# RWKV recurrence with split accumulator banks, low-rank weights scaled by halves, and a new instruction order

## The chip, the cores and the metric

The kernel runs on one core of a Trainium2 chip. The metric is the device time of one execution in microseconds (us); shorter is better. The core's engines are TensorE (PE in the profile, with PEld for its weight loads), VectorE (DVE), ScalarE (ACT), GpSimd (POOL) and SyncE (SP), which issues the transfers between device memory and the on-chip memory. Each engine works off its own queue in order; semaphores tie the queues together. Matrix products land in PSUM, which has eight banks of 512 float32 columns over 128 partitions.

## What is computed

A trunk of four residual layers works on x, 256 tokens by 1024 channels, in float32. Layers 0 and 3 mix tokens by RWKV-7, layer 1 by stick-breaking attention, layer 2 by sparse attention over selected keys; a SwiGLU feed-forward net follows each. The change touches the RWKV layers and the order of everything. Cut to what matters of the reference:

```python
shifted = jnp.pad(h, ((0, 0), (1, 0), (0, 0)))[:, :-1]
xm = h[:, :, None, :] + (shifted - h)[:, :, None, :] * mix
rkv = jnp.einsum('bsjd,jde->bsje', xm[:, :, :3], w_rkv)
logw = -jax.nn.softplus(-(w0 + jnp.tanh(xw @ w1) @ w2)) - 0.5
a = jax.nn.sigmoid(a0 + (xa @ a1) @ a2)
...
def step(state, inp):
    r_t, w_t, k_t, v_t, kk_t, a_t = inp
    sa = jnp.einsum('bhvk,bhk->bhv', state, kk_t)
    state = (state * w_t[:, :, None, :]
             - sa[..., None] * (kk_t * a_t)[:, :, None, :]
             + v_t[..., None] * k_t[:, :, None, :])
    return state, jnp.einsum('bhvk,bhk->bhv', state, r_t)
```

The step runs over 256 tokens in 16 heads of 64 channels.

## The kernel before

**A plan and a table.** The program isn't issued as it is written. `trunk` records every operation in a `Plan`; `schedule` (L478) then reads the order of all operations out of a packed table, `ORDER`, together with the engine of each operation that can run on two (those recorded on `anye`) and the buffer slot of each tile. `emit` (L526) issues them in that order, so that nearly every instruction of the profile has line L547. A turn 0 in the table stands for filler: two matmuls on a constant tile into a PSUM bank of their own, `warm_o` (L1571 to L1573). Unpacked, the table has 6579 turns, of which 35 are filler.

**Buffers.** Of the eight PSUM banks five have the tag `ps`, two the tag `g` (long products), and one is the filler's. Weights arrive in pieces of 512 KB in three buffers, `raw`. Most are split in two on arrival: ACT or DVE rounds a piece to `wh`, DVE subtracts to get the rest, `wl`, and products run over both parts.

**An RWKV layer.** In order of the code:

- The low-rank weights come by one transfer of 512 KB and one of 1536 KB into `lw` (L858). DVE scales the first by two vectors `mu`, 1024 columns each (L871 to L873), and the product `lora_in` runs over eight chunks of channels (L874).
- The sum of squares `ss` over x gives 1/rms (`rstd`). Then, for two chunks at a time, DVE forms h and one difference `dh` over both (L909 to L912), mixes, and the products follow: `kp` (keys), `rp`, `vp`, and the gate `pg`.
- The recurrence runs in four chunks of 64 tokens. Each chunk needs the inverse of a 64 x 64 triangular matrix per head and chunk. DVE inverts the 32 x 32 diagonal blocks (`inv`); transposes bring them to `xd` and `xw`, and four copies per layer go from `xw` into the tile `XT`, 64 columns wide. The lower left block is joined on TensorE in `combine` (L1184), four units per layer: a product into the bank `cmb1`, of which 32 + 32 partitions are copied to `zs` by two copies, and a second product into the bank `cmb2`, whose two halves go to `XT` with sign reversed. Both show as tile `cmb` in the profile.
- `Chain` (L1205) is the recurrence itself, for half of the heads, and is run twice. A step (L1212) is: `pS` (state times keys, two banks, not in the first chunk), DVE adds to `u`, `xu` (inverse times u, one bank), two evictions of 64 partitions each to `UV`, `qu` (update), DVE forms the new state `Sn`, and products into the output `Y`. The two halves of the heads are independent, so that the table can run them beside each other. Y of the second half holds two `ps` banks from its first step to its end. The norm of the output (`vb`) and the output projection (`po`) follow.

In the code, `halves` names the partitions 0 to 63 and 64 to 127: `r` is a half and `rb` the other one.

Of the kernel before, what the change touches and what calls it, by code (L numbers as in the profile page):

```python
# [303 lines left out]
8X(o*M@pQxAdc;WgQwPzs;|4cy1KgRSJj_pDf@3rzsC)(zHZu=qQ!1ZaMNzuZv&S%?WWzdn|9M~aQmj+v@cQPzcs^6yJ=sF{Bo0We&3Jl=7etAO}l9~?WT
PuLvUsDO`RfO371kqpP?Vr(o%0p(f87d56lw-Plyxg2vHFxj}{w7WF=x$+-<|zH*CkSxT$1D$y6knP0KWwzKHo&%ul#}G`8${mU3gBh$hAn*IgC1u-
&+83r`s4f%(-
Bgb`Io;)jMjjGML+rZj#m`s0rH#@3E7wv_Td+K^2t+_K?ROWO*Hv|54lrhJusz|ECc_tK8cpNgbBjvwa^3o>KK1Zfb7s<aZ*p|r>6rVuT8Xb3kNjr9zdJG
NbMJ-1}%6SkYNbFqo*em!m5e%6lLb}Z2z#g6TAq_Nj)NXz+E*0EcCv6iwUTjsA!vt@fZb2a<RnwiPu&42LL-M>#&)28AH6-yTi-
1lTOZLXwb@@LELPh}z^Gp@9L61OZFOPHP?mEIql5vde+B~JpAf`1%kasI~Pf|*aHV9)tG>??}B5d7iALw3$C*u&e8*gZz=ls+fNM1Jp(v3+`&?w&9<W^Bm
V4r9ktcAp)xO@>o!;ra#+@w|zbc-A1QQl`H0Hf~`FarKvodCcbi1rIS(!W1UyCxQMy)-i`3MsYcoLh49k-  # L310
bE9A*J8>n845GsU0$|UMSdmyvOt^8n0`veFdp|mRLEV!6?TE#3NsmoGRcgKgvpfmoJ6=wE;+!GyCfWPr6n{?vx^3!Vf@RJ9|&=@BoC4ABg5S(eT{K6W;kR
6#6DuTi(Ln|SGPK7ZDJdZrcrCKY8~scT&<R|f~7Sq7Ll!>UB|q@EFz}N<s{}4L(Hzm;|#5whZ#T0JtK}R?QSC4+_5|x6*H2Xk|A;?7&vLhunpj=f`V>NBI
Edh#a2w@c_l#b;>hOKvQ)-HrgjBzda~9n8C4a-HJr&4r?KkDWw}>?yjcX!(>(QnC-))2%9C=l%%JqJ-otJYMxFO!xE#SIx?5SSqYWn&B;{bWvnn@N<Si-l
QTGhQo|9^)Z2OTd))|=%jHk?2VD>0jP(iviNxMb35O#l`+!w6J<0v;xeAloT8lc7?DMSTVASDwmp@anSphKGTUEbt02Iq#+1*OIcE+yzqijELs%=u$rib+
7eMGu_A1?vgM_lbJSCJd0|zXTFD(b5K-
OJJ|~l#^q^kWK)^OW+frC)_~*VEZrh&;<3^E48nbf{COCUsb@xo*=<&q~%KZvdnz`shN+iXFgHdw%W9sfg^(!^};&w2{;Nm^)no^B4aE10bu}dO~SZlfCz
my!Kd#i=<YUxM-NF?4|*Grq+fazS|J(e+7u9{L&s<+d22o&0+Ko-ftGE^P**IW2i!KK=vQ3RZ3RiK3G=ij4A=2(0drk8LtRpVF0m1$d_R!21}-
>SEfYYcl(NZ+o+{IK%IkRvPico$c2b8z%%oVjS2W1o3*_dKm&n91j(N6k>9y@1SQZH~)+N|BqDksYv_%eij^ip5NXFG>LWnvxG{81t+hAaTSVc0yU51q`K
<S*pCkF(Sq?SMO)BYz~S$`5&eoT4&4T#D}?MIRGYBf^1SE*ELKdwBiRw}YwcK4tJ#pB|rIDB0ke0NaVd9|}Mv<KgY9jn`Y)z$5+`{v%Gd-wdiR_FHn%)Is
Fj(Pib=JW|WIypK%B3wVPVJ~j&9#p4RHa3ZkV&eJ8H2dJjy4$^%z3sE_8+=PyuGLKN`;7zJ|C{>lI=8-clCk*U^+9AO`OdVztCoM(RYON@sh-  # L320
!hS{=R>fwpUirmC{rP!{9y+Is?uJ2oejTHb~ZomQ^BDYMPu_s_D8Ms|HA`@LGEn#q^z<vg5>OQX`zE$+ai|EdpZ`~7D-
tk1R*+wZY9+idx;u@Si?+v^f*t~V8@WwAC|6EIY(yFIl6m)mA#T-
o2On60wc$gO*u*_v6)Om0UjWfPLwHE`l8Zzr;`tevlAGU|CuMVjV@GQf^>r0FtH2oyX_aM;!HFobU?$V<!;RNb=qs)edx0G9$!Y(`GdHK3yi=pAvnL4FY<
_iG#670y7y`7&iBz)i}RD+qX>#IbZ6*08iw!s0nWGn8R%8T%JS%mXiMX7kw`JjxCrQ-
E}?gOJHU{EZ^7h{xl}c*6Jn9s2m&zKX%nlQJTu18D%8#Vr_WINvWDI%qj19KwkMDJv8;<^~)a1n*Tw?u_D26N6Z)a^9wJI%N%VW}^q{jHYZ#NfOR`8sUL)
P8(R4J)+@^P+-WKjEOG0uK}Drr93x83Y36*4C0cYqAxWl33x`x4U}<dL6|%X0i>@@u+N_VACZs^G>-
9C2O2?kLj<|O?YD7z=l=t4H&}u(FXj=s%^b#Jj71H`<Q5Y#DiR{}5xKSynS_Y<G)*%JxLMrJ+4iwbb+v8R?Lx}NL`IUkW3+EXB8K549K$y(%QD8Rrm0;$8
w5Z%no&pyF4$kWSYkF>07g#ZdNGYg(g5_OPlZfGitmtZzs~S$%2N0vLrVMS@;y(Q5qMV!`6ti5={yxw`&*VcfB#(kh4{ccGmN|9&bxPn_~%bfrTEwuDr$<
Kh$(GF3FDS#Kcp+lo)T>_7GfyQg}B4G+^%$Pb>zDT#^&DR%_)W8_`z6?K59N#HF#eY%<3zCz>oIJ*=g$=YZsHrBQ;*j4l`!D+T*FyH%Bjz^55yK?LXPyH@
<C6i;vEE-fUzNelArxNoCeH8A~<yb}v&OPgrsU7g$SXy;FBP-AUtX(LUOHnw-  # L330
8yKCv4ke|UlS2AQ3++T+ujbpnr4N9Dtm$6H4L6TS>=kcVM^6oKy4E&XASobv~Edy;UPiFZEyz;5_2k{?H&rQur@Ua38YhimP`SH#)HSy2_Ke5G2i%d*DVx
_xl>01i^)<L2&Zb7Eyi$%DQH`CX{^N3b?{7P|xfY2%gGT4`+#w)R$QEpO7fAK&uI{r2=<*OQf;2W1Z`%Mo5HwW>|Nv76(6OZTAYFDeHs>(e|WGCa%H3TmC
zJtzCud5Hh06swDxX+&Z__=O=b^QS8rgXdE}jDR7X52Z9eCdhxSA`rJIMrvjx9bs$9;w4*c*Apww9aezYDT2Y={bRL%nmtqTU3;vGY#?3FKkL;BRS>yYYs
<^5Hj45#h<agAOL1-#@A^EJ1j926G3F|8Wzv!yBMkSz=6sbdX;d9(Y}6s5cIaXtvm7~|T9hS>dciPcnV-6@7>G-
# [1401 lines left out]
```

## Time and profile before

| what | value |
|---|---|
| median of 3 runs | 1362.21 us |
| lowest and highest | 1360.86 and 1362.78 us |
| the profiled execution's own time | 1363.01 us |
| its span in the profile | 1361.2 us |
| read from HBM | 217.08 MB, 160 GB/s over the span |

```profile
DVE  8999898776788988775799998876699998988754
ACT  5856467554235676554356865654249455666532
...
DMA  7332166655554557646646456666642421676554
```

Each digit is the busy share of one fortieth of the span (34 us) in tenths. The first RWKV layer takes the first five slices or so, the second one those from the thirtieth to the thirty-fourth. In both the transfers are light, at the end above all, and DVE is nearly full before the recurrence. Rows of a view by stretches give start and end, length, the busy time of PE, PEld, DVE, ACT and POOL with the count of instructions, the granted clock, the DMA share and GB/s. Rows of a timeline give start and length in us, engine, line, operation, out<-in; `x16` merges 16 instructions in a row. In square brackets stands how long the engine sat idle before and what ended it. Rows of a tile give shortest, median and longest duration in ns. A float32 matmul shows as two instructions, since TensorE takes it in two passes.

### The profile page before, as it was taken

To read this page: it belongs to the slowest core of one execution; us is meant where nothing else is said; L and a number is where in the kernel's file an instruction comes from. 1 tells how busy PE (TensorE), PEld (TensorE's weight loads), DVE (VectorE), ACT (ScalarE), POOL (GpSimd) and SP (SyncE) were. 2 spreads that over 40 slices of the span, in tenths; PEclk is the share of its full clock that TensorE was granted. 3 is DMA by queue.
4 is the path that set the end of the run, shared out by engine and by line. 5 is a ranking of instruction groups with operands and counts; after the bars stand their busy time and mean duration, and the time that the engine had idled before them with its cause. 6 is when DMAs were issued, how large, how long until landed. Compare 5 with 4: busy or idle time off the path is not lost.

```text
span 1361.2 us, 25699 instructions
## 1 busy us (share of the span) xinstructions
PE 1347.9 (99%) x10382; PEld 1179.9 (87%) x10382; DVE 1129.4 (83%) x1898; ACT 748.7 (55%) x1266; POOL 8.9 (1%) x18
## 2 busy tenths in 40 slices
PE   9999999999999999999999999999999999999998
PEld 8887898888888998888998788888898878988887
DVE  8999898776788988775799998876699998988754
ACT  5856467554235676554356865654249455666532
POOL 0000000000000000000000000000000000000000
PEclk9999999999999999999999999999999999999999
DMA  7332166655554557646646456666642421676554
GB/s 246 126 118 78 50 206 213 189 181 157 189 171 124 153 174 227 193 152 185 189 140 196 141 175 193 206 194 208 186 144 79 137 70 50 200 209 198 178 167 131
DMA packets 62854, 221.88 MB, mean 163 GB/s; under 512 B 7312, under 2 KB 8592, under 8 KB 62480
## 3 DMA queue, kind: packets, MB, share of 16 engines
q1 hardware_dynamic: 62736, 220.25, 52.2%
q8 instruction: 81, 1.33, 0.4%
q14 instruction: 37, 0.30, 0.1%
HBM read 217.08 MB, written 1.05 MB: 160 GB/s over the span
## 4 chain that ended last, share of the span: by engine, by line
PE 90%; DVE 4%; DMA 4%; ACT 1%; issue 1%; SPq 0%; DVEq 0%; ACTq 0%
PE gate L547 17%; PE dn L547 17%; PE up L547 17%; PE po L547 6%; PE qk L547 5%; PE vp L547 4%; PE kp L547 3%; DMA raw<-in_wts_dram 3%; PE rp L547 3%; PE vps L547 2%; PE z L547 2%; PE Y L547 1%; PE lora_in L547 1%; PE pg L547 1%; DVE wl L547 1%
## 5 line engine op out<-in xcount | busy, mean ns | idle before, releaser
L547 DVE TENSOR_TENSOR wl<-raw,wh 128x1024 fp32r<-128x1024 f32 x285 | 348.1, 1223 | 92.7 <-ACT wh L547 90.0
L547 ACT CAST wh<-raw 128x1024 fp32r<-128x1024 f32 x231 | 242.0, 1049 | 196.9 <-PE dn L547 110.5
L547 PE MATMUL dn<-h,wh 128*128 128x512 f32 x704 | 244.3, 390 | 0.0
L547 PE MATMUL dn<-h,wl 128*128 128x256 f32 x704 | 198.7, 282 | 0.2 <-DVE wl L547 0.2
L547 PEld LDWEIGHTS dn<-h,wh 128*128 128x128 f32 x704 | 132.2, 188 | 27.6
L547 PE MATMUL gate<-xg,wring 128*128 128x512 f32 x704 | 134.9, 336 | 0.8 <-DVE wring L547 0.5
L547 PEld LDWEIGHTS dn<-h,wl 128*128 128x128 f32 x704 | 133.1, 189 | 0.7 <-DVE wl L547 0.5
L547 PE MATMUL up<-xg,wring 128*128 128x512 f32 x704 | 132.2, 336 | 0.0
L547 DVE TENSOR_TENSOR wring<-raw,wring 128x1024 fp32r<-128x1024 f32 x88 | 107.6, 1222 | 29.6 <-ACT wring L547 27.2
L547 PE MATMUL gate<-xg,wh 128*128 128x512 f32 x352 | 125.5, 392 | 0.5 <-DVE gus L547 0.5
L547 PE MATMUL up<-xg,wh 128*128 128x512 f32 x352 | 125.4, 392 | 0.0
L547 PEld LDWEIGHTS gate<-xg,wring 128*128 128x128 f32 x704 | 107.4, 188 | 16.0 <-DVE wring L547 0.8
L547 PEld LDWEIGHTS up<-xg,wring 128*128 128x128 f32 x704 | 107.5, 188 | 14.6
L547 ACT CAST wring<-raw 128x1024 fp32r<-128x1024 f32 x85 | 89.3, 1051 | 46.1 <-DMA raw<-in_wts_dram 17.4
L547 PE MATMUL gate<-xg,wl 128*128 128x256 f32 x352 | 98.4, 280 | 0.0
L547 PE MATMUL up<-xg,wl 128*128 128x256 f32 x352 | 98.4, 280 | 0.0
L547 PE MATMUL qk<-xg,wh 128*128 128x256 f32 (+1 forms) x384 | 91.8, 320 | 0.0
L547 PEld LDWEIGHTS gate<-xg,wh 128*128 128x128 f32 x352 | 66.1, 188 | 15.3 <-DVE gus L547 0.8
L547 PEld LDWEIGHTS up<-xg,wh 128*128 128x128 f32 x352 | 66.1, 188 | 14.5
L547 PE MATMUL qk<-xg,wl 128*128 128x256 f32 x256 | 71.8, 280 | 0.4 <-DVE wl L547 0.3
L547 PEld LDWEIGHTS qk<-xg,wh 128*128 128x128 f32 x384 | 63.6, 188 | 6.3 <-issue 0.8
L547 PEld LDWEIGHTS gate<-xg,wl 128*128 128x128 f32 x352 | 66.1, 188 | 0.0
(325 smaller groups left out, 2620.5 us busy)
## 6 DMA issues: line engine op xcount, KB each, us to landing
raw<-in_wts_dram SPq DMA_DIRECT2D x397, 512.0 KB, 3.7
lora<-in_lora_dram SPq DMA_DIRECT2D x2, 1536.0 KB, 9.3
rhl<-qa SPq DMA_DIRECT2D x32, 64.0 KB, 3.1
xt<-in_xT_dram SPq DMA_DIRECT2D x4, 256.0 KB, 3.8
lora<-in_lora_dram SPq DMA_DIRECT2D x2, 512.0 KB, 4.8
lg<-in_lora_dram SPq DMA_DIRECT2D x8, 128.0 KB, 5.0
inv<-in_id_dram SPq DMA_DIRECT2D x2, 512.0 KB, 3.3
out_dram<-xt SPq DMA_DIRECT2D x4, 256.0 KB, 4.3
```

The lines of the kernel that those rows point to most:

```text
L547: getattr(getattr(nc, o.eng), method)(*map(real, args), **{k: real(a) for k, a in kw.items()})
```

## The change

1. `ORDER` is replaced; unpacked it has 6564 turns, 26 of them filler. Its positions in the table: 22 before the first real product (20 before), 2 and 2 in the two recurrences (5 and 10 before). Each transfer was given a wide margin when this order was sought.
2. The filler's own bank is gone: `ps` has six banks, and a filler turn writes to the `ps` bank that has been free longest. If none is free, the turn is left out.
3. The scaling of the low-rank weights runs in halves, four instructions of 512 columns instead of two of 1024, the first four chunks of channels first.
4. `dh` of the first two chunks is formed one by one.
5. The second transpose writes straight into the right half of `XT`; two copies per layer instead of four bring the upper blocks to the left half. `xw` is gone.
6. In `combine` the first product makes all 64 columns, so that one copy of 128 partitions replaces two of 32; the second product has a bank for each half.
7. `xu` has a bank for each half.

```diff
-        for o in ops:
+        left = {b: set(b.ops) for b in self.bufs if b.group == "ps"}
+        of, held = collections.defaultdict(list), {f"ps_{k}": (-1, None) for k in range(6)}
+        for b in left:
+            for o in b.ops:
+                of[o].append(b)
+        for n, o in enumerate(ops):
             if o is None:
-                warmer()
+                free = [(at, tag) for tag, (at, b) in held.items() if b is None]
+                if free:
+                    warmer(min(free)[1])
                 continue
+            for b in of[o]:
+                left[b].discard(o)
+                held[b.slot] = (n, b if left[b] else None)
...
-        for i in range(2):
-            m = mu[:, i].rearrange("p i c -> p c i")[:, :, :, None].to_broadcast([P, NC, 2, 64])
-            dve.tensor_tensor(w1a1[1 + i], w1a1[0], m, op=ALU.mult)
+        for c in range(0, NC, 4):
+            for i in range(2):
+                m = mu[:, i].rearrange("p i c -> p c i")[:, c:c + 4, :, None].to_broadcast([P, 4, 2, 64])
+                dve.tensor_tensor(w1a1[1 + i][:, c:c + 4], w1a1[0][:, c:c + 4], m, op=ALU.mult)
...
-            dve.tensor_tensor(dh[:, c:c + 2], h[:, c:c + 2, :S], h[:, c:c + 2, 1:], op=ALU.subtract)
+                if c == 0:
+                    dve.tensor_tensor(dh[:, i], h[:, i, :S], h[:, i, 1:], op=ALU.subtract)
+            if c > 0:
+                dve.tensor_tensor(dh[:, c:c + 2], h[:, c:c + 2, :S], h[:, c:c + 2, 1:], op=ALU.subtract)
...
-        xw = T([32, 32], "wh", "xw")
-        dve.transpose(xw.rearrange("p u t -> p t u"), XI)
-        for g in (1, 3, 0, 2):
-            r = slice(g * 32, (g + 1) * 32)
-            anye.copy(XT[r, :, g % 2 * 32:g % 2 * 32 + 32], xw[r])
+        dve.transpose(XT[:, :, 32:].rearrange("p u t -> p t u"), XI)
+        for r in (slice(0, 32), slice(64, 96)):
+            anye.copy(XT[r, :, :32], XT[r, :, 32:])
...
-            z, zs, z2 = bank("cmb1"), t1("zs"), bank("cmb2")
+            z, zs, z2 = bank("cmb1"), t1("zs"), (bank("cmb2"), bank("cmb2"))
...
-                        pe.matmul(z[hi:hi + 32, c * 32:(c + 1) * 32], SB[k][lo:hi, lo // 64, c0 + c // 4, c % 4, 0, 32:],
+                        pe.matmul(z[lo:lo + 64, c * 32:(c + 1) * 32], SB[k][lo:hi, lo // 64, c0 + c // 4, c % 4, 0, :],
                                   x[lo:hi, c], start=True, stop=True)
-            for hi in (32, 96):
-                anye.copy(zs[hi:hi + 32], z[hi:hi + 32, :S])
+            anye.copy(zs, z[:, :S])
...
-                        pe.matmul(z2[lo:hi, c * 32:(c + 1) * 32], zs[hi:hi + 32, c * 32:(c + 1) * 32],
-                                  xr_[hi:hi + 32, c], start=True, stop=True)
+                        pe.matmul(z2[lo // 64][lo:hi, c * 32:(c + 1) * 32], zs[hi:hi + 32, c * 32:(c + 1) * 32],
+                                  X[hi:hi + 32, c, 32:], start=True, stop=True)
             for lo in (0, 64):
-                anye.scale(X[lo:lo + 32, :, 32:], z2[lo:lo + 32, :S].rearrange("p (c t) -> p c t", c=2 * NCH), -1.0)
+                anye.scale(X[lo:lo + 32, :, 32:], z2[lo // 64][lo:lo + 32, :S].rearrange("p (c t) -> p c t", c=2 * NCH), -1.0)
...
-                a = bank("xu")
+                a = bank("xu"), bank("xu")
...
-                            pe.matmul(a[r, q * C:(q + 1) * C], XT[r, 4 * p0 + 4 * c + q, :], u0[r, q, :],
+                            pe.matmul(a[hh][r, q * C:(q + 1) * C], XT[r, 4 * p0 + 4 * c + q, :], u0[r, q, :],
                                       start=True, stop=True)
                 for hh, r, rb in halves:
-                    anye.scale(UV[hh][r, p0:p0 + 4, c, :], v3(a[r, :4 * C], 4), -1.0)
+                    anye.scale(UV[hh][r, p0:p0 + 4, c, :], v3(a[hh][r, :4 * C], 4), -1.0)
...
-    plan.emit(nc, {"ps": 5, "g": 2, "xm": XMS, "raw": RAWS, "wh": 3, "wl": 3, "t": TS, "t2": 5},
+    plan.emit(nc, {"ps": 6, "g": 2, "xm": XMS, "raw": RAWS, "wh": 3, "wl": 3, "t": TS, "t2": 5},
```

More of the change, by code (lines that the diff above doesn't have):

```diff
@@ L309 @@
[L309 to L334, printed above, removed]
@@ new lines @@
+cgg11Sy#8Km!wqCdOvm<;-Lw9&5%Q9ytKNM6N9DYp%C-
+D_UQg$AAyct4x)^6dOZuwJWi9ygtdp17_zyFG;5jn3rFMObJHB18tz0Z5|A=#6yeH(B1efCZb8d?lob#ugKe%<DKj8eF?rw8>cFIrq{wY7={DANAU7Em0d
+z<GQPdMM_7xdHP$9%0z<EP!X`A(0I&d>Sc1De@g!JF7YY|dc|{|Ot2Q&R(++Nu3L_OXIkLM$N8WA=wxoT<i$5r*_6#4Muip@a0>w4}n~H=0wzQn^x<V?n!
+-P<L$+Mk1hJ-+AekU6e&D?_$=;#<8EtWPrP80rP!iE)zDh1lNoSDF!!g9Lv9Y>n$e40poj&v7N6owmo7a>Q)D=-
+)C%|t*x;&m#wa>GP~Pl%NFY_;Ov}Y9oCv@wOO09db3eyY>GK@c7>JO{iQZ5HCYE)Ueubo2CHOQtppWj=R=kU$a;!pm_6q)0A(?$Gt`+w@JL+fGKfLJhAcC
+|3f!sl4{TktSlCwEN;EuA9=c3%atfgS%~)hQ87qR8CAFtj=Rr-
@@ new lines @@
+#zRx6ViA(flVkqE(@TVt)*c0%CJaP*RhN@>O!FZXV?>@-
+q#90DV{RFf}z#pY3x=znh^xZNTqn`hd82bEYF!UMzyy*LjQ~nBYyZ@Vj+w&&(3nRi(TtgR~h&nz}uxHDR2b_Df6)!CrDJf+zNsF5YXWof{3~iaLB})LE1p
+9u0Y&`@K`6Q&%C41*QP|D*~;<{|?jJ%^n8}lxpQBXij{HawV94?b`DlnbbkX0&!85v6UEi!G6@Cm>dr6u9JN(lR}#rqbeDbCAhj<CP+_)}q9u4P-
+|!@GCIKc872=-
+c9!5;xygUpx7Rke@nQ<SqF<VNvZNZwe*#kyw{P?TW4#(Rzb(vfvGIyLT+!pIMU!;>pUM=w39pn@d|?Z7$wXcN_hN>RIb8ad7nXK<|HDbej)$mTR^8uqNg{
+L3L8)YbTY~%F+Ilmi+o|xdHb_^{of^>D-
+{+>EFrC_R8|`ciYbnBsL%IHh1v1abfF0?hL2$eVoDd%E{W{+S3mY5E~D7z09_E;bE3Qe>Ujhg@2SkjPP*3i)U)*kZ*IQ*g($~#nz^?o?qK$IrdSO>BZmIO
@@ new lines @@
+<L4}4Btx;|Jyp5u{ARFMiT&(Q?FXJ>UGAcgs&K@h85`EZcG&(tUcN$h(aktxrFErMnvQX(xRce*!3xf#yO)BD8K0ll~$;;ePE>~u53{P5+JF>F}oT6~`37
+L@NPh;N8?ZfQTGK0)k#-NG+Y!|#B0Dq7NPq=#-
+{><TEc>~W<;clqyC(0UH1&gBY+r<B_7F1CQu}R6_t_|KJi%xaZvJMC(o`c%<@_8oTp%4=3ZLS!S;HKc?pq>)q@u6+oY=hR>)~33FO;e+!)lKq>NNps6OAO
+&*3cPD{*+G0n!~-g*;F;PnfomwG(d^qGcGAGLNyQiw+rS^EfvcCqEqrnvw>~>=(Z!%Ll<A{3KBp{NxKb9)r)AO49k3Q&l|&0yOQJVvlP-
+r$!dXJwd7btbW#QE-R~h(>hU0HD$X;vdeG=X22Td>ieWRK2RJ)(q(v{5)X*c<d7oLnyey&VsFyUdmNqUz|zRJw!YzuGPrW~-
+>SV$jS?*7KC3D@Iq#wIdMB%1IKuT=JV4SrU=<8_mvvHIYDA-=ljL?>g7Tx$7JF>pnqiQ?E*<-
@@ new lines @@
+=8GK3i{}EkUZCOTD}?<<%2>#oL=p!z;l*U*0Q5G&!5s#>RTQYC-IkX}lu;c?A57_U6B~B)i?9WvC=coQIEDKoS<mQYBDKH{3XwkY+YP5*Kt!`4*rcbfaKS
+6r4sF3WUj7npeun_xKb|&j6HQf|+!PnRU!E+++hxm_?-dGQ^WBOBtaxgeht$F(;NNCnb78>7PWi7;%Tm<^-%%XenaWytt;-
+Br%lCqCr7h(*h)eH2v`=B4H8`C&z*uxum#9>q()xl!l(RAVMK&OWHv)L<SRoG1xP{pLiN7O)4UV7~#RZ^8sT(6c<zV8g<erz}T!X(M@{Jm`qE62x&Vr%{(
+)!m`4-y`M*r#lT(1p^GJfptA5f;UnjkOU}G1-
+gndkUS5TL+OUaaZv6)JmPBtBLv^X($b3(`xm1AngW&%zoBtDd$dZJ!A8IU5Gn%ICz`4h3wXb>l$F_sup<|eQRIAJywQWBGinU1|R(RpIIV?7!&IrcHbDqb
+FuS&}Ey6CM0&rm<A%6ZA-
@@ L1570, in trunk @@
     nc.vector.memset(wx, 1.0)
-    wo = psum.tile([P, 512], F32, name="warm_o")
-    plan.emit(nc, {"ps": 5, "g": 2, "xm": XMS, "raw": RAWS, "wh": 3, "wl": 3, "t": TS, "t2": 5},
-              lambda: [nc.tensor.matmul(wo[:, :S], wx[:, :P], wx, start=True, stop=True) for _ in range(WARMERS)])
+    plan.emit(nc, {"ps": 6, "g": 2, "xm": XMS, "raw": RAWS, "wh": 3, "wl": 3, "t": TS, "t2": 5},
+              lambda tag: [nc.tensor.matmul(psum.tile([P, 512], F32, name="warm_o", tag=tag, bufs=1)[:, :S], wx[:, :P], wx, start=True, stop=True)
+                           for _ in range(WARMERS)])
 def _rows(w, r0, nr, c0, n):
```

79 lines of the change are left out of this document (41 added, 38 removed).

## The prediction

> **What bounds the kernel now.** I read the page first, then the busy times by stretch, then the waits, then the order of instructions at the places that the change touches.
>
> ```profile
> span 1361.2 us, 25699 instructions
> PE 1347.9 (99%) x10382; PEld 1179.9 (87%) x10382; DVE 1129.4 (83%) x1898; ACT 748.7 (55%) x1266; POOL 8.9 (1%) x18
> PEclk9999999999999999999999999999999999999999
> PE 90%; DVE 4%; DMA 4%; ACT 1%; issue 1%; SPq 0%; DVEq 0%; ACTq 0%
> ...
> 20.00:117.00 97.00, 97.00 (x795) 84.91 (x794) 94.74 (x187) 61.81 (x105) 4.37 (x5) 1.00 0.43 134
> 117.00:161.00 44.00, 42.84 (x1075) 33.50 (x1076) 37.95 (x85) 22.71 (x45) 0.00 (x0) 1.00 0.15 48
> ...
> 508.00:669.00 161.00, 161.00 (x931) 142.15 (x930) 120.82 (x163) 80.80 (x121) 0.00 (x0) 1.00 0.61 185
> ...
> 1100.00:1152.00 52.00, 50.32 (x1178) 39.69 (x1178) 43.99 (x93) 30.41 (x60) 0.00 (x0) 1.00 0.18 64
> ```
>
> TensorE is the bound nearly everywhere: 90% of the chain that ended last, never short of clock, and in a feed-forward stretch (508 to 669) not idle at all. No edit there can give anything unless it takes matmuls away, and this change takes none. What can be won is time in which TensorE waits or is fed filler. The stretches above (start and length, then busy time of PE, PEld, DVE, ACT, POOL) show two such places besides the start: the two recurrences of the RWKV layers, where PE lacks 44.00 - 42.84 = 1.16 us and 52.00 - 50.32 = 1.68 us. Beside this idle time stands the filler, matmuls on a constant tile:
>
> ```profile
> L1573 PE MATMUL warm_o<-warm_x x70: 272/273/421, 1.2 to 1130.9; 128*128 128x256 bf16 x70
> ...
> 1.20 6.73 PE L1573 MATMUL warm_o<-warm_x 128*128 128x256 bf16 x40 [1.20 <-DVE warm_x L1570]
> ...
> 1125.09 0.83 PE L1573 MATMUL warm_o<-warm_x 128*128 128x256 bf16 x6
> 1125.85 0.68 PE L547 MATMUL xu<-u,XT 64*64 64x64 f32 x16
> ```
>
> Forty of the 70 stand before the first real work, so 30, or 15 turns of two, lie in the recurrences. Six take 1125.85 - 1125.09 = 0.76 us, a turn thus 0.25 us and all 15 turns 3.8 us. With the idle time, 3.8 + 1.16 + 1.68 = 6.6 us is all that the two recurrences can give back without fewer matmuls.
>
> **The xu product in two banks.** Does it make TensorE faster?
>
> ```profile
> 106.55 10.63 PE L547 MATMUL vp<-xv,raw 128*128 128x256 f32 x48
> 117.11 0.71 PE L547 MATMUL qct<-consts,QC 64*128 64x64 f32 x16
> ...
> 143.37 0.46 PE L547 MATMUL pS<-Sn,PR 64*64 64x64 f32 x16
> 143.65 0.63 PE L547 MATMUL Y<-PR,Sn 64*64 64x64 f32 x16
> 144.12 0.63 PE L547 MATMUL xu<-QC,XT 64*64 64x64 f32 x16
> 144.61 0.68 PE L547 MATMUL xu<-u,XT 64*64 64x64 f32 x16
> ```
>
> From start to next start, 48 full passes of 256 columns take 117.11 - 106.55 = 10.56 us: 0.22 us each, so 0.055 us for 64 columns and 0.88 us for 16 passes in a row. One xu unit takes 0.49 us (144.12 to 144.61), so its two halves already run beside each other in one bank. pS, whose passes use all four pairs of partition halves, takes 0.28 us. The xu edit leaves each half on its own partitions, in and out. Bounds for the matmuls: nothing, or 0.49 - 0.28 = 0.21 us in each of 16 units (two layers, two halves of the heads, four chunks), 3.4 us. I take nothing, because the unit is already near half of 0.88. The Trainium skill ("TensorEngine Tiling (Array Packing)", Gotcha 1: PSUM Pressure) says that different row tiles can't use one PSUM bank at the same time. By that rule the split would let the halves meet; the 0.49 us here says that they meet already, so it is only a rival below.
>
> What the second bank does change is the evictions:
>
> ```profile
> 1131.88 0.38 ACT L547 ACTIVATE UV<-xu 64x256 f32<-64x256 f32 x1 [1.17 <-PE xu L547]
> 1132.29 0.43 DVE L547 TENSOR_SCALAR UV<-xu 64x256 f32<-64x256 f32 x1 [1.01 <-ACT UV L547]
> ```
>
> DVE waits 1.01 us for ACT's read of the other half of the same bank: in one bank the two evictions go one after the other, 0.38 or 0.43 us each. In two banks they can go side by side, about 0.4 us off the path from xu to qu, in 16 units. It costs no instruction. If one engine is at a cast, the half waits for it and nothing is won. The Trainium skill ("PSUM — Partial Sum Buffer", PSUM bank collisions raise a hardware error) lets two engines work in different quadrants of one bank at once; by that rule one bank would do and this term would be nothing. The wait above stands in the program all the same, so I keep the row.
>
> **The joining products and the inverse's tiles.**
>
> ```profile
> L547 DVE COPY XT<-xw x7: 671/682/691, 125.8 to 1116.2; 32x1024 f32<-32x1024 f32 x7
> L547 DVE STREAM_TRANSPOSE xw<-inv x2: 1977/1991/2005, 121.1 to 1109.8; 128x1024 f32<-128x1024 f32 x2
> ...
> L547 ACT COPY zs<-cmb x11: 362/364/365, 126.3 to 1130.0; 32x256 f32<-32x256 f32 x11
> L547 DVE COPY zs<-cmb x5: 416/418/431, 126.9 to 1130.3; 32x256 f32<-32x256 f32 x5
> L547 ACT ACTIVATE XT<-cmb x10: 372/374/375, 129.7 to 1135.3; 32x256 f32<-32x256 f32 x10
> L547 PEld LDWEIGHTS cmb<-xd,SB x256: 101/108/108, 125.5 to 1127.3; 32*32 32x32 f32 x128
> ...
> L547 PEld LDWEIGHTS xu<-u,XT x192: 129/135/135, 138.9 to 1147.3; 64*64 64x64 f32 x192
> ```
>
> Removed: four of the eight XT copies (4 x 0.68 = 2.7 us, seven of the eight on DVE) and 8 of the 16 zs copies (8 x 0.37 to 0.42 = 3.1 us on both engines); the one zs copy that is left has 128 partitions instead of 32 and the same 256 columns. The transpose stays, 1.99 us, with its output spread over XT; no row shows that spread, I take no change and keep 2 x 1.99 us of DVE as the upper end (it comes after the inverse, with pg products on PE as cover). Per joining unit the path loses one zs copy (0.39 us) and, with the second product in two banks, one XT half (0.37 us). The first product's weights grow from 32 to 64 columns. Its load takes 108 ns now, xu's with 64 columns 135 ns: 27 ns more, either hidden behind the streaming (nothing) or shown 16 times in each of 8 units (3.5 us). I take nothing, since two matmuls run beside each other; the upper end stays in the range.
>
> If everything were exposed, the path would lose 16 x 0.4 + 8 x (0.39 + 0.37) = 12.5 us, but only 6.6 us can be got. How much is? The unpacked order table puts 26 filler turns where the old one has 35; before the first real work 22 instead of 20, in the recurrences 4 instead of 15. That is 11 turns x 0.25 = 2.8 us that the table no longer needs to fill. Of the idle 2.8 us, gaps like this one end when UV comes sooner:
>
> ```profile
> 152.44 0.46 PE L547 MATMUL pS<-Sn,PR 64*64 64x64 f32 x16 [0.52 <-DVE Sn L547]
> ...
> 1112.34 3.45 PE L547 MATMUL pg<-sg,lg 128*128 128x256 f32 x16 [0.75 <-ACT gT L547]
> ```
>
> while the other one has nothing to do with the change. I count a quarter of the idle time, 0.7 us. **Recurrences: 3.5 us**, between 0 and 6.6. What is late next is DVE (37.95 of 44 us): the removed copies come off DVE too, which is why I think that the gain isn't swallowed there.
>
> **The start.**
>
> ```profile
> 3.08 6.12 DMA xt<-in_xT_dram
> ...
> 7.83 2.36 DVE L547 TENSOR_TENSOR lora<-lora,mu 128x1024 f32<-128x1024 f32 x2 [0.48 <-DMA lora<-in_lora_dram]
> 9.99 1.13 PE L547 MATMUL ss<-sq,ones 128*128 128x256 f32 x4 [1.20 <-ACT sq L547]
> 10.96 7.07 PE L547 MATMUL lora_in<-xt,lora 128*128 128x256 f32 x32
> 15.02 0.88 DVE L547 SCALAR_TENSOR_TENSOR pre<-xt,vecs,rstd 128x256 f32<-128x256 f32 x2
> 15.93 0.69 DVE L547 TENSOR_TENSOR pre<-pre 128x512 f32<-128x512 f32 x1
> 16.66 0.48 DVE L547 SCALAR_TENSOR_TENSOR xm<-pre,vecs 128x256 f32<-128x256 f32 x1
> 17.68 0.80 PE L547 MATMUL kp<-kx,wh 128*128 128x256 f32 x2
> ```
>
> The last part of x lands at 9.20 and sets ss; PE waits 1.20 us before it. Scaling the weights by halves ends the first half after 1.2 us, at 9.0, instead of both at 10.2: about 0.9 us of lora_in fits into PE's wait, and lora_in ends that much sooner. kp also needs xm. With dh for the first chunk alone, h (0.44) and half a dh (at least 0.35) stand before xm instead of 0.88 + 0.69: 0.4 to 0.8 us sooner, I take 0.7, near the halved row. Both paths must shorten; the lesser counts, **0.7 us**, between 0 (the weights' transfer ahead of x delays the last x by as much) and 0.9. In the second RWKV layer lora_in keeps PE full meanwhile: nothing. Three more DVE instructions per layer cost overhead only where DVE isn't waiting anyway.
>
> **Sum.** 3.5 + 0.7 = 4.2 us off. The profiled execution took 1363.01 us (span 1361.2), so 1358.8 for it; the median of the runs shown, 1362.21, is 0.8 below, which gives **1358.0 us**. About 0.2% (2.7 us) can be told from no change.
>
> **The rivals.**
> - **The filler goes, the waiting stays** (1362.2 - 0.7 = 1361.5 us). Filler needed no shared bank before; now it needs a free one of six, of which xu and the second join take two each. Four turns may then mean that no bank was free, not that TensorE was needed. For: DVE is busy 94.74 of 97 us up to the recurrence. Against: the shorter evictions above.
> - **Banks run out** (slower). The sixth bank is used up by the second of xu; a unit that needs two waits until an eviction pair ends, 0.8 us. Place: 16 xu and 8 join units. The point is five such waits (4.2 / 0.8): there the gain is gone; from nine it is slower by over 0.2%; with 12 of 24, 1358.0 + 9.6 = 1367.6 us. For: while the second half of the heads runs, its Y holds two of the six for the whole recurrence, and xu and pS take the other four. Against: before, xu and pS took all three that Y left of five, so nothing is scarcer than it was.
> - **Waits on transfers go too.** The wider margin could remove TensorE's few waits for weights:
>
> ```profile
> PE vp L547 <- DMA raw<-in_wts_dram: 1.6, 2, 1.2
> ...
> PE gate L547 <- DVE wring L547: 0.5, 1, 0.5
> PE qk L547 <- DVE wl L547: 0.3, 1, 0.3
> ```
>
>   Together 2.4 us: 1355.6 us. Against: three raw buffers can't be filled before they are free. The same table could also move work wrongly in the feed-forward stretches, where PE has no idle time to gain; how it orders them I can't read, so I give that no time of its own.
> - **Two banks speed up xu's matmuls**: 3.4 us more, 1354.6 us; the times above speak against it.
>
> **How the numbers follow.** Forecast 0.48, filler only 0.22, banks 0.12, transfers 0.13, faster xu 0.05. About 0.08 of the forecast's own spread (1355 to 1360.5) lies within 0.2%. Faster 0.40 + 0.13 + 0.05 = 0.58; same 0.22 + 0.08 = 0.30; slower 0.12. The range goes down to 1362.2 - 6.6 - 0.7 - 2.4 = 1352.5, and up to 1361.5 + 3.5 = 1365: all 6.6 us of the recurrences and the transfers at the one end, the filler rival with the full price of the wider weights at the other. It leaves out the banks' 0.12 and a little of the rest.
>
> **What would show it.** Right: UV's halves overlap on ACT and DVE; xu keeps 0.49 us; 12 XT and zs copies fewer; filler in the recurrences 8 matmuls and PE's idle time there below 2.8 us; first kp near 17.0. Wrong: the first join unit takes longer than the second; xu or join units wait for evictions; the recurrences last as long as before, or a feed-forward stretch has gaps that it hadn't.

## The result, and the profile after

| | median | lowest to highest | ratio to before (95%) |
|---|---|---|---|
| before, 6 runs | 1362.26 us | 1360.41 to 1363.74 | |
| after, 6 runs | 1369.79 us | 1367.09 to 1376.60 | 1.0062 (1.0044 to 1.0079) |

The changed kernel is slower by 0.6%, 7.5 us; the prediction was 4.2 us faster. The profiled execution took 1367.67 us. Its page, from the span, the busy times and the chain that ended last:

```profile
span 1365.9 us, 25685 instructions
PE 1356.0 (99%) x10364; PEld 1182.6 (87%) x10364; DVE 1130.4 (83%) x1913; ACT 728.5 (53%) x1245; POOL 8.2 (1%) x18
PE 99%; DVE 1%; issue 0%; ACT 0%
```

DMA's 4% of the chain before and most of DVE's 4% are gone, and still the span is 4.7 us longer. TensorE is now nearly the whole chain, so it must be TensorE itself that takes longer over something. The timeline of the changed kernel shows where:

```profile
1.20 18.74 PE L1585 MATMUL warm_o<-warm_x 128*128 128x256 bf16 x44 [1.20 <-DVE warm_x L1583]
...
8.59 2.51 DVE L559 TENSOR_TENSOR lora<-lora,mu 128x512 f32<-128x512 f32 x4 [1.00 <-DMA lora<-in_lora_dram]
...
20.00 3.78 PE L559 MATMUL ss<-sq,ones 128*128 128x256 f32 x8
23.57 7.45 PE L559 MATMUL lora_in<-xt,lora 128*128 128x256 f32 x32
30.67 0.59 PE L559 MATMUL kp<-kx,wh 128*128 128x256 f32 x2
```

The 44 filler matmuls last from 1.20 to 20.00, 0.427 us each; before, 40 of them began at 1.20 and the first real product at 7.77, 0.164 us each. The scaled weights (`lora`) were ready at 11.1. Filler, meant for time in which nothing is ready, holds up real work: the first `kp` starts at 30.67 instead of 17.68, 13.0 us late.

Behind the start the changed kernel is faster. Rows by stages, each from the first `kp` or `gate` product to the next (first RWKV layer; everything between; second RWKV layer). Before, then after:

```profile
17.68:185.73 168.05, 166.90 (x2089) 144.54 (x2087) 159.06 (x314) 103.61 (x183) 4.80 (x5) 1.00 0.38 118
185.73:999.68 813.95, 811.65 (x5032) 714.86 (x5031) 664.61 (x1069) 436.39 (x747) 0.77 (x3) 1.00 0.59 181
999.68:1173.61 173.93, 170.53 (x2130) 146.38 (x2129) 161.35 (x311) 104.37 (x189) 2.46 (x4) 1.00 0.31 96
```

```profile
30.67:198.13 167.46, 166.43 (x2083) 145.55 (x2081) 154.65 (x310) 99.95 (x180) 3.70 (x5) 1.00 0.38 121
198.13:1008.73 810.60, 810.52 (x5033) 715.09 (x5031) 672.79 (x1091) 423.31 (x731) 0.60 (x3) 1.00 0.60 182
1008.73:1178.34 169.61, 168.59 (x2115) 146.77 (x2113) 156.94 (x304) 102.79 (x190) 3.03 (x4) 1.00 0.31 99
```

The lengths stand before the comma, PE's busy time behind it. The stages change by -0.6, -3.3 and -4.3 us, and the rest (to the end of the span) by 0.0: 8.3 us won, 13.0 lost, +4.7 in all. In the middle stage PE's idle time falls from 2.30 us (813.95 - 811.65) to 0.08. The list of PE's waits in the changed kernel has three rows left, none of them for a transfer or a weight:

```profile
PE warm_o L1585 <- DVE warm_x L1583: 1.2, 1, 1.2
PE pS L559 <- DVE Sn L559: 0.7, 2, 0.5
PE vb L559 <- ACT ysq L559: 0.5, 1, 0.5
```

**Why filler became slow.** By the list of changes a filler turn writes to the `ps` bank that has been free longest. How it gets that bank stands in the last lines of the change (cut):

```diff
-    wo = psum.tile([P, 512], F32, name="warm_o")
...
-              lambda: [nc.tensor.matmul(wo[:, :S], wx[:, :P], wx, start=True, stop=True) for _ in range(WARMERS)])
+              lambda tag: [nc.tensor.matmul(psum.tile([P, 512], F32, name="warm_o", tag=tag, bufs=1)[:, :S], wx[:, :P], wx, start=True, stop=True)
+                           for _ in range(WARMERS)])
```

`psum.tile` is called for every matmul. Each call is a new tile in a slot that has one buffer, so that the earlier tile must be released first, and what releases it is the end of the matmul that wrote it. The program's list of TensorE instructions shows the wait (first before, then after):

```
1 L1573 LDWEIGHTS warm_x [waits DVE_49]
2 L1573 MATMUL warm_o<-warm_x 128x256
3 L1573 LDWEIGHTS warm_x
4 L1573 MATMUL warm_o<-warm_x 128x256
```

```
1 L1585 LDWEIGHTS warm_x [waits DVE_49]
2 L1585 MATMUL warm_o<-warm_x 128x256
3 L1585 LDWEIGHTS warm_x
4 L1585 MATMUL warm_o<-warm_x 128x256 [waits PE_49]
```

`PE_49` is TensorE's own semaphore: a matmul waits for the one before it to be complete, where otherwise they stream one behind the other. The matmuls of the changed kernel start 0.43 us apart. In the profile the row of this tile shows no such wait, only longer instructions: a median of 371 ns, against 273 before.

```profile
L1585 PE MATMUL warm_o<-warm_x x52: 269/371/395, 1.2 to 1132.7; 128*128 128x256 bf16 x52
```

### The profile page after: what moved, and what is told of

It reads as the page before. It is cut to its first block, busy times and chain, and to the rows that moved or that the text cites. A ratio compares the mean times of both kernels' runs of the same rounds, so it can differ in the third digit from the quotient of the medians.

```text
span 1365.9 us, 25685 instructions
## 1 busy us (share of the span) xinstructions
PE 1356.0 (99%) x10364; PEld 1182.6 (87%) x10364; DVE 1130.4 (83%) x1913; ACT 728.5 (53%) x1245; POOL 8.2 (1%) x18
## 3 DMA queue, kind: packets, MB, share of 16 engines
HBM read 217.08 MB, written 1.05 MB: 160 GB/s over the span
## 4 chain that ended last, share of the span: by engine, by line
PE 99%; DVE 1%; issue 0%; ACT 0%
PE gate L559 18%; PE dn L559 18%; PE up L559 18%; PE po L559 7%; PE qk L559 6%; PE vp L559 4%; PE rp L559 3%; PE kp L559 3%; PE vps L559 3%; PE z L559 2%; PE warm_o L1585 1%; PE sc L559 1%; PE lora_in L559 1%; PE Y L559 1%; PE cmb L559 1%; PE pg L559 1%
## 5 line engine op out<-in xcount | busy, mean ns | idle before, releaser
L559 ACT CAST wh<-raw 128x1024 fp32r<-128x1024 f32 x219 | 229.3, 1049 | 171.8 <-PE dn L559 90.9
L559 PE MATMUL up<-xg,wring 128*128 128x512 f32 x704 | 139.8, 335 | 0.0
L559 PE MATMUL gate<-xg,wring 128*128 128x512 f32 x704 | 138.3, 336 | 0.0
L559 ACT CAST wring<-raw 128x1024 fp32r<-128x1024 f32 x76 | 79.9, 1051 | 36.8 <-issue 16.8
L559 ACT COPY gus<-gate 128x256 f32<-128x256 f32 x88 | 32.3, 373 | 71.0 <-PE gate L559 68.5
```

Source lines behind the costliest of these rows:

```text
L559: getattr(getattr(nc, o.eng), method)(*map(real, args), **{k: real(a) for k, a in kw.items()})
```

## The experiments

The theory: the new tile for each filler matmul costs the start 13 us, and the rest of the change is worth about 8. The rival: the change loses elsewhere (wider joining products, banks, the order), and the slow filler only fills time that would be idle anyway. All experiments but two start from the first one, called **keep** here; kernels "measured together" ran one after the other on the same chip. The code cuts leave out what isn't changed; each run's other lines are those of the kernel it starts from.

### One tile for as long as the bank stays the same: keep

```diff
-                    warmer(min(free)[1])
+                    warmer(min(free))
...
+    spare = {}
+    def warmer(key):
+        if spare.get("key") != key:
+            spare.update(key=key, tile=psum.tile([P, 512], F32, name="warm_o", tag=key[1], bufs=1))
+        for _ in range(WARMERS):
+            nc.tensor.matmul(spare["tile"][:, :S], wx[:, :P], wx, start=True, stop=True)
```

> The changed kernel with one edit: a filler turn that goes to the same bank as the turn before, with nothing else in that bank between, writes to the same tile instead of a new one. Theory A (each new tile makes a filler wait for the one before): the 44 fillers at the start come every 0.165 us as before the change, not every 0.427 us; the first real product starts near 8.5 us instead of 20.0, the first kp near 19 instead of 30.7, and the time falls by about 11.5 us to near 1356 us, below the kernel before. Rival B (the 8.35 us that the change won behind the start are only made-up delay: a late start lets the weights run ahead): the start is repaired as well, but the waits for weights come back and the time stays at 1361 to 1363 us. Rival C (the fillers only fill time in which the data is late anyway): time stays at 1367 us.

Measured: 1354.62 us (1353.82 to 1355.44), ratio 0.9946 (0.9932 to 0.9959). From its timeline:

```profile
1.20 6.86 PE L1590 MATMUL warm_o<-warm_x 128*128 128x256 bf16 x44 [1.20 <-DVE warm_x L1583]
...
8.11 2.00 PE L559 MATMUL ss<-sq,ones 128*128 128x256 f32 x8
...
9.94 7.20 PE L559 MATMUL lora_in<-xt,lora 128*128 128x256 f32 x32
...
16.79 0.47 PE L559 MATMUL kp<-kx,wh 128*128 128x256 f32 x1
...
1122.97 0.63 PE L559 MATMUL xu<-QC,XT 64*64 64x64 f32 x16
1123.44 0.63 PE L559 MATMUL xu<-u,XT 64*64 64x64 f32 x16
```

As many filler matmuls, now 0.157 us each (1.20 to 8.11), and the whole loss is gone: 15.2 us between the medians of after and keep, 13.1 us between the spans (1365.9 and 1352.8). One edit of the tile's lifetime turns the sign of the change. (2.1 us of the 15.2 are executions of the changed kernel at a lower clock, see the last section.) The first `kp` comes 13.9 us earlier than in the changed kernel (16.79 instead of 30.67): 11.9 of it is the shorter filler.

The clock is part of the price too. In keep the first fillers start 0.21 us apart and the last ones 0.11, and the trace's records of the granted clock begin at 5.1 us, with 1.00. In the changed kernel the fillers start 0.43 us apart to the end, the records begin only at 24.3 us, and the eight `ss` products behind the fillers take 3.57 us (20.00 to 23.57), against 1.83 here (8.11 to 9.94). In oldnew and few_new, below, the records begin 4.4 and 4.3 us after the first real product. So the waiting filler seems to leave the clock low, which costs 1.7 us more at `ss`. That the clock is low until then is read from these times: the clock column of the profile shows 1.00 where it has no record. At full clock, in the recurrences, a filler matmul takes 0.33 us with a new tile (the changed kernel) and 0.11 without (keep).

The stages of keep:

```profile
16.79:184.98 168.19, 166.92 (x2082) 146.45 (x2081) 155.59 (x311) 100.76 (x181) 3.68 (x5) 1.00 0.38 123
184.98:995.62 810.64, 810.57 (x5032) 715.24 (x5031) 672.97 (x1091) 423.05 (x730) 0.83 (x3) 1.00 0.59 182
995.62:1165.30 169.68, 168.71 (x2114) 147.09 (x2113) 157.04 (x304) 102.76 (x190) 3.05 (x4) 1.00 0.31 99
```

Against before: start -0.9, first RWKV layer +0.1, middle -3.3, second RWKV layer -4.3, the end -0.1; together -8.4 us of span. Cut also at the last `vp` product, the stretches from there to the first `gate` hold the recurrences. In the two layers they are, before and in keep:

```profile
116.80:185.73 68.93, 67.78 (x1279) 57.56 (x1277) 62.20 (x124) 40.61 (x76) 0.00 (x0) 1.00 0.28 84
1104.20:1173.61 69.41, 67.73 (x1272) 57.52 (x1271) 61.45 (x115) 40.37 (x78) 0.00 (x0) 1.00 0.25 77
```

```profile
115.91:184.98 69.07, 68.19 (x1272) 59.26 (x1271) 58.30 (x117) 39.44 (x76) 0.00 (x0) 1.00 0.26 79
1096.28:1165.30 69.02, 68.05 (x1272) 58.60 (x1271) 58.43 (x111) 40.16 (x79) 0.00 (x0) 1.00 0.25 78
```

They change by +0.14 and -0.39 us only. In the second layer one unit of `qct`, 0.64 us, stands ahead of this cut in the kernel before and behind it in keep. So of the 4.3 us won in the second layer 3.9 lie ahead of its recurrence.

### Only the new tiles, in the kernel before: oldnew

```diff
-    wo = psum.tile([P, 512], F32, name="warm_o")
...
-              lambda: [nc.tensor.matmul(wo[:, :S], ...
+              lambda: [nc.tensor.matmul(psum.tile([P, 512], F32, name="warm_o", tag="warm", bufs=1)[:, :S], ...
```

> The kernel before with one edit: each filler matmul gets a new tile in the filler's own bank. Theory A: 40 fillers at the start at 0.427 instead of 0.165 us, so 10.5 us later first real product (near 18.3 us), and up to 30 x 0.26 = 7.8 us more in the recurrences as far as they stand on the path; time 1370 to 1380 us. Rival C (fillers are cover for late data): no change, 1362 us.

Measured together with keep: 1375.59 us (1375.30 to 1375.96), ratio 1.0100 (1.0086 to 1.0113), 13.6 us slower. The filler has its own bank here, as before, and no other part of the change is in. TensorE's timeline of this kernel:

```profile
1.20 17.04 PE L1572 MATMUL warm_o<-warm_x 128*128 128x256 bf16 x40 [1.20 <-DVE warm_x L1570]
18.03 3.62 PE L547 MATMUL ss<-sq,ones 128*128 128x256 f32 x8
...
28.65 0.59 PE L547 MATMUL kp<-kx,wh 128*128 128x256 f32 x2
```

`kp` starts 11.0 us late (28.65 - 17.68) with 40 matmuls at 0.42 us. The new tile alone does it: neither a shared bank, nor the order, nor the banks' number is needed.

### Fewer filler turns at the start: few_new and keep_few

```diff
+        skip = 5
         for n, o in enumerate(ops):
+            if o is None and skip and n > 15:
+                skip -= 1
+                continue
```

The same edit, five of the 22 turns at the start left out, once in the changed kernel (few_new) and once in keep (keep_few).

> The changed kernel itself, each filler on a new tile, but with 17 instead of 22 filler turns at the start. By theory A each of the ten matmuls left out is worth 0.427 us: first real product at 15.7 instead of 20.0, time 4.3 us below the changed kernel's undisturbed runs (1367), so 1363. If something other than the fillers holds the start: no change.

> The first run's kernel with 17 instead of 22 filler turns at the start (34 matmuls instead of 44). At 0.165 us each they end at 6.8 instead of 8.1 us; the sum of squares is ready for TensorE only near 7.7 us (the first run's DVE adds end at 7.0 and its square of the last part at 8.2). If the fillers still stand in the way: 0.3 to 0.5 us faster. If what follows waits for the low-rank weights (landed at 9.0) anyway: no change, within 0.3 us. If the clock needs them: slower by over 1 us with a lower granted clock.

Measured together: few_new 1367.65 us (1364.03 to 1368.45), 1.0038 (1.0024 to 1.0052); keep_few 1354.27 us (1353.50 to 1354.43), 0.9944 (0.9931 to 0.9956). In few_new `kp` starts at 26.40 instead of 30.67: ten matmuls less are 4.3 us, 0.43 each. The medians show only 2.1 us of this, and not the 4.3 that were expected. Three of its four executions had a lower granted clock (last section); the fourth, at 1364.03, is 3 us or more below the executions of the changed kernel at full clock (1367.09 and up). In keep_few ten matmuls less can't be told from none: there the filler only covers time before the data arrive. So a filler turn at the start is free as long as it ends before the data arrive, and costs its full length beyond.

### Which edits bring the rest: keep_xu1, keep_cm1, keep_ones, keep_copies

```diff
-                            pe.matmul(a[hh][r, q * C:(q + 1) * C], XT[r, 4 * p0 + 4 * c + q, :], u0[r, q, :],
+                            pe.matmul(a[0][r, q * C:(q + 1) * C], XT[r, 4 * p0 + 4 * c + q, :], u0[r, q, :],
...
-                    anye.scale(UV[hh][r, p0:p0 + 4, c, :], v3(a[hh][r, :4 * C], 4), -1.0)
+                    anye.scale(UV[hh][r, p0:p0 + 4, c, :], v3(a[0][r, :4 * C], 4), -1.0)
```

keep_xu1 is this edit: `xu` in one bank again. keep_cm1 does the same for the second joining product (`z2[lo // 64]` to `z2[0]`), keep_ones does both. keep_copies gives the removed copies back: each XT copy is issued twice, each zs copy as two of 64 partitions.

> The first run's kernel with xu back in one bank for both halves (the order unchanged). If the second bank wins by letting the two UV evictions overlap, they come one after the other again and the recurrences are longer by up to 16 x 0.4 = 6.4 us, of which I expect 1 to 3 us to show; xu units keep 0.49 us. If two banks speed up the matmuls (the rule on row tiles), xu units take longer than 0.49 us. If the second bank does nothing: within 0.5 us of the first run.

> The first run's kernel with the second joining product back in one bank. If the overlap of the two XT evictions counts: up to 8 x 0.37 = 3 us longer, I expect 0 to 1.5 us. If not: within 0.5 us of the first run. The second product keeps 0.62 us per unit in both.

> The first run's kernel with xu and the second joining product both back in one bank. Alone they made no more than 0.4 us. If the overlap of evictions is worth nothing here, within 0.7 us of the first run; if one stands in for the other, 1 to 3 us slower.

> The first run's kernel with as many copies as before the change: each XT copy is done twice on its engine, and each zs copy in two halves of 64 partitions one after the other. That adds 4 x 0.7 and 8 x 0.4, 6 us of work on DVE and ACT in the two recurrences. If the recurrences became shorter because these copies went: 2 to 4 us slower than the first run. If it was the new order (and the copies are covered): within 1 us of it.

| | median (lowest to highest) | ratio to before (95%) | against keep |
|---|---|---|---|
| keep_xu1 | 1355.05 us (1354.45 to 1356.01) | 0.9949 (0.9936 to 0.9961) | +0.4 |
| keep_cm1 | 1354.40 us (1353.88 to 1355.44) | 0.9944 (0.9932 to 0.9957) | -0.2 |
| keep_ones | 1355.63 us (1355.07 to 1356.19) | 0.9957 (0.9943 to 0.9970) | +1.0 |
| keep_copies | 1356.35 us (1355.55 to 1361.05) | 0.9964 (0.9951 to 0.9977) | +1.7 |

The first two can't be told from keep, with which they were measured; the 1 to 3 us expected of keep_xu1 didn't come. The last two were measured at other times, so their differences to keep are uncertain by some tenths; keep_ones stands 1.4 us above keep_few, with which it was measured, and their ranges don't meet. Both splits together are thus worth about 1 us. keep_copies falls between its two expectations, so that it decides for neither; as it issues both copies on one engine, 1.7 us is rather an upper bound of what the twelve copies are worth. Of the 12.5 us that the prediction counted if everything were exposed, some 3 at most are real.

### The first joining product with 32 columns of weights: keep_narrow and narrow_few

```diff
-                        pe.matmul(z[lo:lo + 64, c * 32:(c + 1) * 32], SB[k][lo:hi, lo // 64, c0 + c // 4, c % 4, 0, :],
+                        pe.matmul(z[hi:hi + 32, c * 32:(c + 1) * 32], SB[k][lo:hi, lo // 64, c0 + c // 4, c % 4, 0, 32:],
                                   x[lo:hi, c], start=True, stop=True)
             anye.copy(zs, z[:, :S])
+            plan.ops[-1].twice = [(zs[hi:hi + 32], z[hi:hi + 32, :S]) for hi in (32, 96)]
```

`twice` makes `schedule` issue the copy as two of 32 partitions each, on the engine that the one would have had. narrow_few is keep_narrow with the edit of keep_few.

> The first run's kernel with the first joining product back to 32 weight columns and its copy back to two copies of 32 partitions, one after the other on the engine that the order names. The wide product took 1.05 us per unit on the chip, the narrow one 0.62. If TensorE is the bound there, 8 x 0.43 = 3.4 us come back at most; the second zs copy costs up to 8 x 0.39 = 3.1 us on the path from the first to the second product. Theory W (TensorE's longer unit counts): 1 to 3 us faster than the first run. Rival (the copy counts as much, or both are covered): within 0.7 us of it.

> The first run's kernel with the narrow first joining product (1352.7 us alone) and 17 instead of 22 filler turns at the start (0.3 us alone, not told from noise). If they add up: 1352.4 us, the fastest so far.

Measured: keep_narrow 1352.74 us (1351.28 to 1353.11), 0.9932 (0.9919 to 0.9944); narrow_few, measured later, 1352.09 us (1351.19 to 1353.23), 0.9927 (0.9916 to 0.9939). The wider weights cost 1.9 us against keep, 1.5 against keep_few, with which keep_narrow was measured, although keep_narrow has eight copies more. From the last `vp` to the first `gate` its two layers take 66.83 and 68.09 us, 3.2 us less than in keep. narrow_few is the fastest kernel of the study, although it can't be told from keep_narrow: 9.6 us below before (1361.66, measured with it) and 17.7 below the change. Its timeline in the second recurrence, then that of the changed kernel:

```profile
1114.16 0.69 PE L565 MATMUL cmb<-xd,SB 32*32 32x32 f32 x32
...
1114.78 0.46 PE L565 MATMUL pS<-Sn,PR 64*64 64x64 f32 x16
...
1116.19 0.69 PE L565 MATMUL cmb<-XT,zs 32*32 32x32 f32 x32
...
1116.81 0.68 PE L565 MATMUL xu<-u,XT 64*64 64x64 f32 x16
```

```profile
1115.82 1.96 DVE L559 STREAM_TRANSPOSE XT<-inv 128x1024 f32<-128x1024 f32 x1
...
1116.88 1.12 PE L559 MATMUL cmb<-xd,SB 32*64 32x32 f32 x32
...
1117.93 3.45 PE L559 MATMUL pg<-sg,lg 128*128 128x256 f32 x16
...
1121.32 0.69 PE L559 MATMUL cmb<-XT,zs 32*32 32x32 f32 x32
...
1121.94 1.76 PE L559 MATMUL pg<-sg,lg 128*128 128x256 f32 x8
...
1132.42 0.42 DVE L559 TENSOR_SCALAR UV<-xu 64x256 f32<-64x256 f32 x1
1132.46 0.38 ACT L559 ACTIVATE UV<-xu 64x256 f32<-64x256 f32 x1 [0.28 <-PE xu L559]
```

From start to next start, the first unit (`cmb<-xd,SB`) takes 0.62 us with 32 columns (1114.16 to 1114.78) and 1.05 with 64 (1116.88 to 1117.93); the second unit takes 0.62 in both. The rows of the tile in the changed kernel show what else grew and what fell:

```profile
L559 PEld LDWEIGHTS cmb<-xd,SB x256: 127/133/133, 137.6 to 1133.9; 32*64 32x64 f32 x128
...
L559 ACT COPY zs<-cmb x5: 372/372/374, 143.8 to 1134.2; 128x256 f32<-128x256 f32 x5
```

A load shows as 133 ns against 108 before, and the whole of this difference appears in the unit's length. The streamed columns are 32 in both, so the loads, not the streaming, set its pace. The wider copy costs no more than the narrow one did.

### The start as it was: keep_start2

```diff
-                m = mu[:, i].rearrange("p i c -> p c i")[:, c:c + 4, :, None].to_broadcast([P, 4, 2, 64])
-                dve.tensor_tensor(w1a1[1 + i][:, c:c + 4], w1a1[0][:, c:c + 4], m, op=ALU.mult)
+                s = 0 if c == 0 else NC - 1
+                m = mu[:, i].rearrange("p i c -> p c i")[:, s:, :, None].to_broadcast([P, NC - s, 2, 64])
+                dve.tensor_tensor(w1a1[1 + i][:, s:], w1a1[0][:, s:], m, op=ALU.mult)
...
-                if c == 0:
+                if c == 0 and j == 1:
                     dve.tensor_tensor(dh[:, i], h[:, i, :S], h[:, i, 1:], op=ALU.subtract)
+                elif c == 0 and i == 0:
+                    dve.tensor_tensor(dh[:, 0, :1], h[:, 0, :1], h[:, 0, 1:2], op=ALU.subtract)
+                elif c == 0 and i == 1:
+                    dve.tensor_tensor(dh[:, 0:2], h[:, 0:2, :S], h[:, 0:2, 1:], op=ALU.subtract)
```

The scaling runs over all chunks at once and `dh` of the first layer over both chunks; stubs of one chunk or one column keep the number of instructions, so that the order table still fits. An earlier form of this edit, keep_start, gave no time.

> The first run's kernel with the start of the first layer undone: the low-rank weights scaled whole (two instructions of 1024 columns, then two short ones, in both layers), and dh of the first two chunks formed together. In the first run lora_in begins at 9.9 us, as soon as the first half is scaled (from 9.05). If the halves are worth what they seem, lora_in begins near 11.2 and the first kp near 18.0 instead of 16.8, and up to 1.2 us of it reaches the end. If DVE's chain to the first kp sets the start anyway: no change, within 0.4 us.

Measured: 1354.20 us (1353.31 to 1355.39), 0.9941 (0.9928 to 0.9954): the same as keep. Its timeline has what was undone:

```profile
10.93 0.70 PE L559 MATMUL lora_in<-xt,lora 128*128 128x256 f32 x2 [0.58 <-DVE lora L559]
...
18.46 0.59 PE L559 MATMUL kp<-kx,wh 128*128 128x256 f32 x2
```

`kp` starts 1.67 us later than in keep, the last `kp` product 0.89 (43.24 against 42.35), the first `gate` only 0.5 us (185.47 against 184.98), and the span is 1352.8 in both. The start's edit moves the start, and nothing of it that could be told from the scatter reaches the end. Besides, `kp` starts at 16.79, 17.38, 17.50 and 17.91 in the profiles of keep, keep_ones, keep_copies and keep_xu1, which share the start's code: 0.7 us of it couldn't be told from this scatter.

### New tiles only in the recurrences: mid_new

```diff
+            if key[0] >= 0:
+                spare["tile"] = psum.tile([P, 512], F32, name="warm_o", tag=key[1], bufs=1)
             nc.tensor.matmul(spare["tile"][:, :S], wx[:, :P], wx, start=True, stop=True)
```

Only the eight filler matmuls of the two recurrences get new tiles.

> The first run's kernel, but the 8 filler matmuls in the recurrences each get a new tile again, as in the changed kernel; the 44 at the start keep theirs. Some executions of the changed kernel had a granted clock of 0.996 and took 4 to 9 us more; those of the first run did not. If the waits between the fillers of the recurrences bring the clock down: some executions of this one have a granted clock of 0.996 to 0.998 and take 3 to 8 us more. If the slow fillers at the start, or the place of the work in time, do it: all stay within 1.5 us of 1354.6 with the clock at 0.999 or 1.000; the eight fillers by themselves cost 8 x 0.26 = 2.1 us at most.

Measured: 1357.03 us (1354.33 to 1359.10, 6 runs), 0.9961 (0.9947 to 0.9975). The three executions at full clock took 1354.33, 1355.23 and 1355.99, about what keep takes; the three others, at 0.997 to 0.999, took 1358.07 to 1359.10. So at full clock the eight tiles cost little by themselves, and nearly all of the loss of the changed kernel at full clock comes from the 44 at the start. The other half of the executions is as the first expectation has it: a lower clock and 3 to 5 us more than keep; whether the waits do it is taken up in the last section.

## Why the prediction was wrong

**The step that failed** is the sentence "before the first real work 22 instead of 20", which entered the sum at nothing, together with "a turn thus 0.25 us", the price of a turn taken over from the kernel before. The two turns more were indeed free (keep, keep_few). What the prediction never asked is whether an instruction that stands in both kernels still costs the same when its destination is made in another way. In the change a filler matmul at the start costs 0.427 us, a turn 0.85, and 44 of them no longer fit before the data: the first `kp`, which the prediction wanted near 17.0, starts at 30.67, 13.0 us late. The edit stood in the diff's last lines; oldnew shows that it costs 13.6 us by itself in the kernel before. The rival on the slower side, banks run out, named another mechanism, and no such wait shows among PE's. The range's upper end missed the median by 4.8 us.

**Without this error**, the other terms can be read from keep, 7.4 us below before by medians, where 4.2 were forecast:

- **Recurrences, 3.5 us.** Mis-sized. The two RWKV layers gained 4.1 us between `kp` and `gate`, but from the last `vp` to `gate`, where the recurrences lie, only 0.25 us, or 0.9 with the unit of `qct` counted back. Ahead of the second recurrence 1.6 us are the transfers' waits of `vp`, which are gone, and 0.6 the unit of `qct`; where the rest comes from wasn't tried. In keep_narrow the same stretches are 3.4 us shorter than before, about the forecast's size: what went missing in keep is mainly the price of the wider weights, below. The filler term held: eight matmuls remain there, as read from the table.
- **xu in two banks.** Right that the matmuls don't change: a unit keeps 0.47 us (1122.97 to 1123.44 in keep). Right that the evictions then run side by side (1132.42 and 1132.46, where DVE had waited 1.01 us). Wrong in size: 16 x 0.4 = 6.4 us were counted as exposed, at most. In keep only 11 of the 16 pairs overlap, by 3.5 us together; in four units the order gives both halves to ACT. And undoing the split costs 0.4 us, not separable from nothing. That the other half of the heads gives TensorE work meanwhile is the likely reason; it was not tried by itself.
- **Joining units and copies.** Twelve copies less, as predicted, and the one zs copy of 128 partitions takes 372 ns (ACT) like one of 32; the transpose into XT takes 1.96 us, so its spread costs nothing. The copies are worth at most about 1.7 us.
- **The wider weights, taken at nothing.** Wrong: the upper end, 8 x 0.43 = 3.4 us of TensorE, was the true one, and 1.5 to 1.9 us of it reached the end. The prediction's own sign is there: the first joining unit takes longer than the second (1.05 against 0.62 us). The Trainium skill ("TensorE: Matmul & The Clock Gate", LDWEIGHTS (loading the stationary operand)) gives the time of a load in ns as about the number of its columns divided by 1.2; an estimate by it is 53 ns for 64 columns and 27 for 32. The trace agrees with the difference: the 32 instructions of a unit run as 16 pairs, two row halves beside each other, and (1.05 - 0.62) / 16 is 27 ns more for each pair. The loads' own rows, 133 and 108 ns, are longer than the rule's times. The prediction had the same 27 ns from the lengths of two loads in the kernel before, and chose the wrong one of its two cases, hidden instead of shown.
- **The start, 0.7 us.** `lora_in` and `kp` did start earlier in keep; none of it that can be told from the scatter reached the end (keep_start2). The prediction asked which of two paths to `kp` is the longer, and not what stands between `kp` and the end of the layer; what takes the gain back there wasn't tried.
- **Waits on transfers go too**, a rival with 0.13: it came true, and by more than its 2.4 us. PE's waits for transfers and weights are gone, and the middle stage alone is 3.3 us shorter. Whether the wide margin or something else in the new order did it was not tried by itself. With the 3.9 us ahead of the second recurrence this is some 7 of the 8.4 us of span between before and keep, and the forecast's sum had nothing for it: that keep is faster, as was forecast, is mostly luck.
- **The filler goes, the waiting stays**, the other rival: true of the first RWKV layer, where PE's idle time was 1.15 us and is 1.27 in keep; not of the second, where it fell from 3.40 to 0.97.

## What to carry to other kernels

When a change moves an instruction's destination to another buffer, ask where that buffer is allocated and how often: a new tile per instruction in a slot of one buffer adds a wait on the instruction before it, and a harmless filler becomes the start's longest chain. Filler is free only while it ends before the data arrive, so check first of all when the first real product starts. In a unit of small products whose loads follow each other, assume that wider weights are paid in full within the unit, and read its price from start to next start.
